# A hybrid layer on one core: earlier raw weight loads, a second state-space input buffer in dead norm roots, other unit spacing, and a down projection that loads one product ahead

## The chip, the core and the metric

The kernel runs on one core of one Trainium2 chip. The metric is the device time of one execution in microseconds (us); several executions are timed and their median is given. The engines are TensorE (PE, its weight loads PEld), VectorE (DVE), ScalarE (ACT), GpSimd (POOL) and SyncE (SP, whose queue issues most DMAs). GpSimd has a DMA queue too.

## What is computed

One layer of a hybrid encoder in float32, for 2048 frames of width 1024. A shared RMS norm feeds one input projection. Half of the mixer is a diagonal complex state-space layer (32 groups of 16 channels, 64 states each), the other half chunked attention with 8 heads, each 64-frame chunk looking at itself and 8 chunks before. Both halves are normalised, joined, projected and added to the residual; a SwiGLU feed-forward (width 2816) and a last norm follow.

```python
h = rmsnorm(x, norm_mix_g)
proj = h @ w_in                                  # u_ssm | q | k | v
y_ssm = s5_mixer(u_ssm, ...)                     # scan over time, then GELU and a sigmoid GLU
y_att = chunked_attention(q, k, v, rel_bias)
x = x + concat(rmsnorm(y_ssm, g1), rmsnorm(y_att, g2)) @ w_out
h2 = rmsnorm(x, norm_ffn_g)
x = x + (silu(h2 @ w_gate) * (h2 @ w_up)) @ w_down
return rmsnorm(x, norm_final_g)
```

## The kernel before

Every float32 product is made of three fp32r matmuls: each operand is split into a high part (a cast on ScalarE) and a low part (a subtraction on VectorE), `split` at L154, and `mm3` at L148 issues hi-hi, hi-lo and lo-hi. So weights that come from memory need a DMA, a cast and a subtraction before their first matmul. `Ordered` (L72) keeps TensorE's instructions in the order in which the program writes them; the other engines' instructions are placed by the framework, by dependence and priority, and each engine then runs its own list in order.

**Stages.** `u_phase` projects the state-space input u and stores it to memory; `att_phase` (L678) runs attention and, between its steps, the query, key and value projections and the state-space units; `mix_phase` (L967) applies GELU, GLU, norms and the output projection; `gate_up_phase` (L1337) and `down_phase` (L1475) are the feed-forward, done with seven products in place of eight per 2x2 block (`B11, T1, T2, B22, T3, B21, T4`).

**Attention's steps.** There are 128 steps (L905): four blocks of 512 frames, four head pairs, two heads, four query tiles. Each step issues scores (L823), the transposes of two steps ago (L855), now and then a product with V (L870), and advances every background unit (L940 to L959). A `Unit` (L656) is a generator with `n` pieces, a first step `s0` and a last `s1`; at each step `advance` (L663) runs so many pieces that the share done is the share of its steps gone, rounded up. `pre` lets a unit's first piece run that many steps ahead; the first piece is the one that loads weights. In block 0 the weights come raw (`load_w`, L684): a 512 KB DMA into one of two `raw` buffers, then `split` into one of three `w` buffers, both in the first piece; later blocks read the already split weights back (`ws`). Units of block 0 start at steps 2, 7, 13 and 19 (`CUT`, L51). GpSimd does only the state-space scan in this stage.

**State-space units** (`ssm_unit`, L557). Eight units of four groups each, 15 steps apart (`SW`, L50, L939), unit b from step 2 + 15b, so the last ends at 122. A unit has 42 pieces. The first loads its input U (eight DMAs of 64 KB, tile `U`, one buffer), `Bst`, eight `Tm` and `Vm` on SyncE (L563 to L577), then passes YL = 8 empty pieces. Two pieces do the input matmuls `pj<-U,Bst` (L585) and eight ScalarE copies into the scan's tile `X` (L588). GpSimd runs the scan (L602 to L614) and moves the states to `XG` with four DMAs (L636). After YX = 9 more empty pieces, two pieces do the output matmuls `pj<-U,Tm` and `pj<-XG,Vm` (L644, L645), which read U again; ScalarE copies the result to Y, which has the same tag and buffer as `X` (L639, L646), and SyncE stores it with eight DMAs (L649). The next unit's U, Tm and Vm can be loaded only after these output matmuls, and its copies into X only after the y stores.

**The norm roots** `rsn` (L1622) are a constant tile of 2048 columns. Columns 0 to 511 are read by block 0's projections (L762), 512 to 1023 by the transposed input of block 1 (L727), at steps 20 to 26; the mix writes it anew (L1211).

**Into the mix.** At step 119 (`OPEN`) the mix's generator is made and loads w_glu (L982); at step 122 (`GSTART`, L946) the state-space pool is released and the mix unit loads y (`yr<-y`, L1024), applies GELU on ScalarE (L1028), splits it (L1031) and begins the GLU matmuls (L1051).

**Down projection.** `group` (L1497) takes up to three feed-forward tiles and runs the seven products in turn. For each it loads two operands of 768 KB on SyncE and splits them (`operand`, L1487; ten `hd` buffers in two pools that lie where feed-forward tiles were), does twelve `mm3` triples (36 matmuls) in four banks and adds the four banks onto accumulators (L1513). The accumulators start as the residual x1: `load_acc` (L1515) loads eight tiles of 512 KB on SyncE, all of them after the operands of the first product. `early` gives the first two products of the first group a high priority. Just before, SyncE's queue carries the stores `hs<-g` of the feed-forward's last tiles (L1434), each of which waits for VectorE.

Of the kernel before, what the change touches and what calls it, by code (L numbers as in the profile page):

```python
# [16 lines left out]
P = 128  # L17
# [5 lines left out]
L = 8  # L23
# [35 lines left out]
MAGIC = 12582912.0  # L59
# [12 lines left out]
class Ordered:  # L72


    def __init__(self, tc):
        self.tc = tc
# [20 lines left out]
def f32(ap):  # L97
    return ap.bitcast(F32)
# [455 lines left out]
    return nb  # L554


def ssm_unit(k, p, psum, S, b, eng):  # L557

    nc = k.nc
    F = GB * CH  # L560
    U = k.t(p, "U", [P, GB, NC])

    def load(out, in_):  # L563
        ins = nc.sync.dma_start(out, in_)
        if b == 0:
            k.tc.keep_in_program_order(ins)

    for j in range(L):
        load(U[j * CH : (j + 1) * CH].rearrange("c g (n t) -> c g n t", n=NSB), S["u"].rearrange("(c g) n j t -> c g n j t", c=CH)[:, GB * b : GB * b + GB, :, j])
    gs = slice(GB * b, GB * b + GB)  # L570
    bst = k.t(p, "Bst", [P, GB, P])
    load(bst[:].rearrange("p g m -> p (g m)"), S["bst"][b // 2][:, (b % 2) * GB * P : (b % 2 + 1) * GB * P])
# [83 lines left out]
class Unit:  # L656


    def __init__(self, gen, n, s0, s1, pre=0, done=0, light=1):
        self.gen, self.n, self.s0, self.s1, self.pre, self.done = gen, n, s0, s1, pre, done  # L660
        self.room = lambda a, b: sum(light if s % 4 == LPH else 1 for s in range(a, b))

    def advance(self, s):  # L663

        if s < self.s0 - self.pre:
            return
        want = 1
        if s >= self.s0:
            want += math.ceil((self.n - 1) * self.room(self.s0, s + 1) / self.room(self.s0, self.s1) - 1e-9)
        if s >= self.s1 - 1:  # L670
            want = self.n + 1
        while self.done < want:
            self.done += 1
            if next(self.gen, self) is self:
                self.done = 1 << 30


def att_phase(k, ident, S, aw, x0, roots):  # L678

    tc, nc, io, pfs = k.tc, k.nc, k.io, k.pfs  # L680
    with ExitStack() as cx:
        hT, vts, qk, keep = {0: tuple(zip(*x0))}, {}, {}, {}

        def load_w(sb, n):  # L684

            w = k.t(aw, "w", [P, 2, 1024], F32R, bufs=WB)
            if sb == 0:
                raw = k.t(aw, "raw", [P, 1024], bufs=2)
                nc.sync.dma_start(raw[:], io["w_qk"][n] if n < 8 else io["w_v"][n - 8])
                for ins in split(k, w[:, 0], w[:, 1], raw[:]):  # L690
                    if n in (0, 4):
                        k.tc.keep_in_program_order(ins)
                keep[n] = w
            else:
                nc.sync.dma_start(f32(w[:]), S["ws"][n])
            return w[:, 0], w[:, 1]

        def keep_w(n):
            if n in keep:
# [30 lines left out]
            yield  # L730

        def qk_unit(sb, pr):
            ws = [load_w(sb, n) for n in (pr, 4 + pr)]
            yield
            hi, lo = hT[sb]
            if (sb, pr) == (0, 0):
# [43 lines left out]
        QK_N = 1 + 2 * KT  # L780

        def v_unit(sb, fh):
            ws = [load_w(sb, 8 + 2 * r + fh) for r in range(2)]
# [143 lines left out]
        for sb in range(NSB):  # L927
            g0 = sb * 32
            C = CUT if sb < NSB - 1 else CUTL
            if sb > 0:  # L930
                if DB:
                    units.append(Unit(hT_unit(sb, 0, DB), 2 + DB, g0 + HTA[0], g0 + HTA[1], 2))
                units += [Unit(hT_unit(sb, DB), 2 + KT - DB, g0 + HTS[0], g0 + HTS[1], HTP), Unit(qk_unit(sb, 0), QK_N, g0 + C[0], g0 + C[1], 3, light=LIGHT)]
            units.append(Unit(v_unit(sb, 0), V_N, g0 + C[1], g0 + C[2], 2, light=LIGHT) if sb else Unit(v0, V_N, *V0, done=1))
            units += [ Unit(qk_unit(sb, 1), QK_N, g0 + C[2], g0 + C[3], 2, light=LIGHT),
                      Unit(qk_unit(sb, 2), QK_N, g0 + C[3], g0 + C[4], 2, light=LIGHT), Unit(v_unit(sb, 1), V_N, g0 + C[4], g0 + C[5], 2, light=LIGHT),
                      Unit(qk_unit(sb, 3), QK_N, g0 + C[5], g0 + C[6], 2, light=LIGHT)]
# [537 lines left out]
def down_phase(k, S):  # L1475
    tc, nc, io = k.tc, k.nc, k.io
    V, te = nc.vector, k.te
    with ExitStack() as cx:
# [5 lines left out]
        def bank(pool):  # L1484
            return k.t(pool, "ps", [P, 512])

        def operand(src, early=False):  # L1487

            g, n = src.shape[0], src.shape[2]
            t = k.t(next(ring), "hd", [P, 2 * DG * 512], F32R)  # L1490
            hi, lo = (t[:, m * g * n : (m + 1) * g * n].rearrange("p (g c) -> p g c", g=g) for m in range(2))
            with tc.high_priority() if early else ExitStack():
                nc.sync.dma_start(f32(lo), src.rearrange("g p c -> p g c"))
            split(k, hi, lo, f32(lo))
            return hi, lo

        def group(hf, f0, g, acc, early):  # L1497

            fs = slice(f0, f0 + g)
            x, y = [bank(dx) for _ in range(4)], None  # L1500
            for n, on_x, first, r, c in ((B11, 1, 1, 0, 0), (T1, 0, 1, 1, 1), (T2, 1, 0, 0, 1), (B22, 0, 0, 0, 1), (T3, 1, 0, 1, 1), (B21, 0, 1, 0, 0), (T4, 1, 0, 1, 0)):
                h = operand(S["hq"][hf, fs, n], early and n in (B11, T1))
                w = operand(S["wc"][fs, n], early and n in (B11, T1))
                if n == B11 and f0 == 0:
                    load_acc(hf, acc)
# [9 lines left out]
        def load_acc(hf, acc):  # L1515
            for i in range(KT):
                a = k.t((a0, a1)[hf], f"acc{i}", [P, HALF])
                nc.sync.dma_start(a[:], S["x1"][i * P : (i + 1) * P, hf * HALF : (hf + 1) * HALF])
                acc.append(a)

        def down(hs, ds, tiles, acc, t0, tn, end):

# [174 lines left out]
```

## Time and profile before

| | |
|---|---|
| timed runs | 2287.0, 2295.97, 2296.15 us, median 2295.97 |
| the profiled execution | 2289.1 us |
| its span, first to last instruction | 2287.1 us, 2.0 us less |
| mean granted TensorE clock | 0.978 |
| moved by DMA | 428.33 MB, 187 GB/s over the span |
| state-space units | between 138 and 700 us |
| passage into the mix | 698 to 716 us |
| feed-forward's end and start of down | about 1830 us |

Times in the profile are microseconds from the span's start. A timeline row gives start, duration, engine, line, operation and `out<-in` by tile names, then a count, and in brackets how long the engine was idle before it and what released it. A row of the waits gives who waited for whom: total, times, longest. "SPq" is SyncE's queue. The releaser named is the last of several by the profile, not always the one that mattered. A row of the windows gives the stretch, its length, busy time of each engine with its count, then TensorE's granted clock, the share of the 16 DMA engines that was busy, and GB/s.

### The profile page before, as it was taken

Reading aid. Unit: us, or ns where it says so; the run is one execution under the profiler, and the core shown is the slowest. Engines: PE = TensorE matmul, PEld = TensorE weight load, DVE = VectorE, ACT = ScalarE, POOL = GpSimd, SP = SyncE. Lnnn points to the kernel's source line nnn. Section 1 sums busy time; section 2 is a strip of 40 time slices with the busy share of each in tenths; the row PEclk is TensorE's granted clock in tenths of the full one; section 3 lists DMA queues with packets and bytes.
Section 4 is the critical chain, followed back from the end, with each engine's and each line's share of the span. In section 5 each row is a group of like instructions: output and inputs, shape, how many; then the busy total and the mean of one; then the engine's idle time right before and its main releaser. Section 6 shows DMA issues by size and latency. Waiting matters only on the chain.

```text
span 2287.1 us, 30278 instructions
## 1 busy us (share of the span) xinstructions
PE 2171.6 (95%) x10632; PEld 1830.1 (80%) x10632; DVE 1544.7 (68%) x2695; ACT 1000.6 (44%) x1654; POOL 348.7 (15%) x813
## 2 busy tenths in 40 slices
PE   8988899999996899999999999999999989999997
PEld 6777688898985788878888887888888778888886
DVE  7755565555556766876776678666666477789776
ACT  6444555455557652343333335333333343344322
POOL 2245765455660000000000000000000000000000
PEclk9998999999998999999999999999999999999999
DMA  8767886666644534854465567555423297465552
GB/s 299 236 221 220 257 223 201 187 188 179 188 132 124 171 121 147 267 189 151 160 200 178 167 211 258 203 169 188 139 96 110 78 341 252 166 212 193 206 189 74
DMA packets 215256, 428.33 MB, mean 187 GB/s; under 512 B 38592, under 2 KB 61168, under 8 KB 208000
## 3 DMA queue, kind: packets, MB, share of 16 engines
q1 hardware_dynamic: 210368, 412.50, 55.3%
q0 software_dynamic: 4736, 13.91, 2.0%
q8 instruction: 83, 1.36, 0.2%
q14 instruction: 69, 0.57, 0.1%
HBM read 286.86 MB, written 129.00 MB: 182 GB/s over the span
## 4 chain that ended last, share of the span: by engine, by line
PE 80%; DVE 6%; DMA 4%; POOL 4%; issue 3%; ACT 1%; SPq 1%; DVEq 0%; POOLq 0%; ACTq 0%
PE X L79 20%; PE ps L79 19%; PE Y L79 10%; PE pf L79 9%; PE big L79 9%; PE W L79 5%; PE pj L79 4%; PE sc L79 2%; PE pt L82 2%; DMA xt<-in_xp 1%; DMA hd<-wc 1%; POOL X L605 1%; DVE lo L156 1%; POOL X L604 1%; POOL st L602 1%
## 5 line engine op out<-in xcount | busy, mean ns | idle before, releaser
L79 PE MATMUL X<-hi,c 128*128 128x512 f32 x1408 | 451.0, 391 | 6.9 <-DVE c L156 5.4
L79 PE MATMUL ps<-hd,hd 128*128 128x512 f32 (+1 forms) x1968 | 430.8, 381 | 6.1 <-ACT hd L156 4.5
L79 PEld LDWEIGHTS ps<-hd,hd 128*128 128x128 f32 x1968 | 358.0, 189 | 77.7 <-ACT hd L156 5.3
L79 PEld LDWEIGHTS X<-hi,c 128*128 128x128 f32 x1408 | 265.3, 189 | 63.4 <-DVE c L156 6.3
L79 PE MATMUL X<-lo,c 128*128 128x512 f32 x704 | 274.9, 391 | 0.0
L156 ACT CAST hd<-hd 128x1536 fp32r<-128x1536 f32 (+1 forms) x106 | 147.7, 1393 | 236.3 <-DMA hd<-hq 178.7
L79 PE MATMUL Y<-hi,c 128*128 128x512 f32 x704 | 224.7, 390 | 1.5 <-DVE u L1389 1.5
L156 DVE TENSOR_TENSOR hd<-hd 128x1536 fp32r<-128x1536 f32 (+1 forms) x106 | 174.4, 1646 | 29.1 <-ACT hd L156 28.4
L156 DVE TENSOR_TENSOR c<-S,c 128x512 fp32r<-128x512 f32 x176 | 121.0, 689 | 98.3 <-ACT c L156 98.0
L1385 ACT COPY u<-X 128x512 f32<-128x512 f32 x132 | 77.4, 587 | 200.7 <-PE X L79 200.7
L1513 DVE TENSOR_TENSOR acc<-acc,ps 128x512 f32<-128x512 f32 x196 | 130.9, 684 | 50.3 <-PE ps L79 47.8
L156 ACT CAST c<-S 128x512 fp32r<-128x512 f32 x176 | 109.4, 622 | 120.1 <-PE Y L79 61.6
L79 PE MATMUL pf<-hi,w 128*128 128x512 f32 x416 | 153.9, 422 | 8.4 <-ACT w L156 4.7
L79 PE MATMUL big<-m,woh 128*128 128x512 f32 x512 | 161.2, 396 | 0.0
L79 PEld LDWEIGHTS Y<-hi,c 128*128 128x128 f32 x704 | 132.5, 188 | 29.9 <-DVE u L1389 2.2
L79 PEld LDWEIGHTS X<-lo,c 128*128 128x128 f32 x704 | 132.8, 189 | 27.5
L156 ACT CAST c<-raw 128x512 fp32r<-128x512 f32 x132 | 82.3, 623 | 150.5 <-PE Y L79 68.5
L79 PE MATMUL Y<-lo,c 128*128 128x512 f32 x352 | 137.2, 390 | 0.0
L868 DVE TENSOR_TENSOR ptl<-pt,pth 128x640 fp32r<-128x640 f32 (+3 forms) x152 | 98.3, 647 | 47.5 <-ACT pth L867 45.9
L852 ACT ACTIVATE s<-s,mn 128x640 f32<-128x640 f32 (+4 forms) x128 | 98.0, 765 | 65.6 <-DVE mn L849 61.1
L867 ACT CAST pth<-pt 128x640 fp32r<-128x640 f32 (+3 forms) x152 | 83.8, 551 | 95.6 <-PE pt L82 91.5
L79 PE MATMUL W<-hi,c 128*128 128x512 f32 x352 | 115.5, 389 | 0.0
(441 smaller groups left out, 4169.9 us busy)
## 6 DMA issues: line engine op xcount, KB each, us to landing
w<-wss SPq DMA_DIRECT2D x36, 1024.0 KB, 6.0
hq<-g SPq DMA_DIRECT2D x140, 256.0 KB, 2.1
hd<-hq SPq DMA_DIRECT2D x42, 768.0 KB, 4.5
hd<-wc SPq DMA_DIRECT2D x42, 768.0 KB, 6.0
raw<-in_w_gate SPq DMA_DIRECT2D x44, 512.0 KB, 3.8
raw<-in_w_up SPq DMA_DIRECT2D x44, 512.0 KB, 4.3
wc<-px SPq DMA_DIRECT2D x66, 256.0 KB, 3.2
wss<-w SPq DMA_DIRECT2D x12, 1024.0 KB, 5.7
```

The costliest lines, as they stand in the source:

```text
L79: return self.tc.keep_in_program_order(self.tc.nc.tensor.matmul(*a, **b))
L82: return self.tc.keep_in_program_order(self.tc.nc.tensor.transpose(*a, **b))
L156: return nc.scalar.copy(hi, raw), nc.vector.tensor_tensor(lo, raw, f32(hi), op=ALU.subtract)
L602: eng.tensor_tensor(t[:, :, :, :n], src, ar, op=ALU.mult)
L604: eng.tensor_tensor(dst, dst, t[:, :, :, :n], op=ALU.add)
L605: eng.tensor_tensor(dst, dst, t2[:, :, :, :n], op=ALU.add)
L852: nc.scalar.activation(s[:, :nk], s[:, :nk], AF.Exp, bias=mn[:], scale=-1.0, accum_out=sums[sb, pr][:, hh, qp : qp + 1])
L867: nc.scalar.copy(pth[:, a:b, qp, :], pt[:, a:b, :])
L868: nc.vector.tensor_tensor(ptl[:, a:b, qp, :], pt[:, a:b, :], f32(pth[:, a:b, qp, :]), op=ALU.subtract)
L1385: nc.scalar.copy(u[:], ps[:])
L1513: V.tensor_tensor(a, a, ps[:], op=ALU.add)
```

## The change

Four things, in the order of the diff.

1. **Spacing.** The units start at the steps in `SU`; the last ends at 119. From unit 2 on, four of the eight empty pieces ahead of the input matmuls are moved behind the scan (`YE`), so that a unit still has 42 pieces.
2. **State-space input.** `ssm_input` loads U and Bst. Units 2, 4 and 6 keep U in `rsn`, the others in tile `U`. For units 2 to 7 it is called from the unit before, two pieces after its XG DMAs; units 0 and 1 load at their own start as before.
3. **Raw weights.** In block 0 the units after the first two issue both raw DMAs four steps ahead (`pre` 4) and split two steps ahead (`mid` 2), where both were done two steps ahead.
4. **Down projection.** In a half's first group the operands of product m + 1 are loaded before the matmuls of product m. In the very first group they are issued on GpSimd's queue (`aside`). The residual comes in quarters (`load_acc(hf, acc, r, c)`, four DMAs of 256 KB), each ahead of the first product that adds to it.

```diff
-SW = 15
+SU = 2, 19, 34, 48, 62, 76, 91, 105, 119
+YE = 4
...
+def ssm_input(k, p, S, b):
+
+    U = S["rsn"][:, : GB * NC].rearrange("p (g c) -> p g c", g=GB) if b > 1 and b % 2 == 0 else k.t(p, "U", [P, GB, NC])[:]
+    bst = k.t(p, "Bst", [P, GB, P])
+    for j in range(L):
+        src = S["u"].rearrange("(c g) n j t -> c g n j t", c=CH)[:, GB * b : GB * b + GB, :, j]
+        yield U[j * CH : (j + 1) * CH].rearrange("c g (n t) -> c g n t", n=NSB), src
+    yield bst[:].rearrange("p g m -> p (g m)"), S["bst"][b // 2][:, (b % 2) * GB * P : (b % 2 + 1) * GB * P]
+    k.ssm_in = U, bst
...
-    for j in range(L):
...
+    if b < 2:
+        for out, src in ssm_input(k, p, S, b):
+            load(out, src)
+    U, bst = k.ssm_in
...
-    for _ in range(YL):
+    for _ in range(YL if b < 2 else YL - YE):
         yield
...
-    for _ in range(YX):
+    for n in range(YX if b < 2 else YX + YE):
+        if n == 2 and 1 <= b < NG // GB - 1:
+            for out, src in ssm_input(k, p, S, b + 1):
+                nc.sync.dma_start(out, src)
         yield
...
-        want = 1
+        want = 1 if self.mid is None or s < self.s0 - self.mid else 2
         if s >= self.s0:
-            want += math.ceil((self.n - 1) * self.room(self.s0, s + 1) / self.room(self.s0, self.s1) - 1e-9)
+            want += math.ceil((self.n - want) * self.room(self.s0, s + 1) / self.room(self.s0, self.s1) - 1e-9)
...
+        def load_ws(sb, ns):
+            raws = [load_raw(n) for n in ns] if sb == 0 else []
+            if raws and ns not in ((0, 4), (8, 10)):
+                yield
+            ws = []
+            for i, n in enumerate(ns):
+                w = k.t(aw, "w", [P, 2, 1024], F32R, bufs=WB)
+                if raws:
+                    for ins in split(k, w[:, 0], w[:, 1], raws[i][:]):
...
-            units += [ Unit(qk_unit(sb, 1), QK_N, g0 + C[2], g0 + C[3], 2, light=LIGHT),
...
+            for gen, n, c in ((qk_unit(sb, 1), QK_N, 2), (qk_unit(sb, 2), QK_N, 3), (v_unit(sb, 1), V_N, 4), (qk_unit(sb, 3), QK_N, 5)):
+                units.append(Unit(gen, n, g0 + C[c], g0 + C[c + 1], 2, light=LIGHT) if sb else Unit(gen, n + 1, C[c], C[c + 1], 4, light=LIGHT, mid=2))
         for b in range(NG // GB):
-            units.append(Unit(ssm_unit(k, sp, psum, S, b, k.ssm_eng), SSM_N, 2 + int(SW * b), 2 + int(SW * (b + 1)), light=SL))
+            units.append(Unit(ssm_unit(k, sp, psum, S, b, k.ssm_eng), SSM_N, SU[b], SU[b + 1], light=SL))
...
-                nc.sync.dma_start(f32(lo), src.rearrange("g p c -> p g c"))
+                (nc.gpsimd if aside else nc.sync).dma_start(f32(lo), src.rearrange("g p c -> p g c"))
...
+            if f0 == 0:
+                acc += [k.t((a0, a1)[hf], f"acc{i}", [P, HALF]) for i in range(KT)]
+                load(0)
+            seen = set()
+            for m, (n, on_x, first, r, c) in enumerate(order):
+                load(m + 1 if f0 == 0 else m)
+                if f0 == 0 and (r, c) not in seen:
+                    seen.add((r, c))
+                    load_acc(hf, acc, r, c)
+                h, w = ops.pop(n)
...
+        def load_acc(hf, acc, r, c):
+            for i in range(4 * r, 4 * r + 4):
+                cs = slice(hf * HALF + c * 512, hf * HALF + (c + 1) * 512)
+                nc.sync.dma_start(acc[i][:, c * 512 : (c + 1) * 512], S["x1"][i * P : (i + 1) * P, cs])
```

More of the change, by code (lines that the diff above doesn't have):

```diff
@@ L560, in ssm_unit @@
     F = GB * CH
-    U = k.t(p, "U", [P, GB, NC])
     def load(out, in_):
@@ L656, with __init__ @@
 class Unit:
-    def __init__(self, gen, n, s0, s1, pre=0, done=0, light=1):
-        self.gen, self.n, self.s0, self.s1, self.pre, self.done = gen, n, s0, s1, pre, done
+    def __init__(self, gen, n, s0, s1, pre=0, done=0, light=1, mid=None):
+        self.gen, self.n, self.s0, self.s1, self.pre, self.done, self.mid = gen, n, s0, s1, pre, done, mid
         self.room = lambda a, b: sum(light if s % 4 == LPH else 1 for s in range(a, b))
@@ L682, in att_phase, with load_raw @@
         hT, vts, qk, keep = {0: tuple(zip(*x0))}, {}, {}, {}
[L684 to L696, printed above, removed]
+        def load_raw(n):
+            raw = k.t(aw, "raw", [P, 1024], bufs=2)
+            nc.sync.dma_start(raw[:], io["w_qk"][n] if n < 8 else io["w_v"][n - 8])
+            return raw
+        def load_ws(sb, ns):
[7 more added lines that the diff above has]
+                    for ins in split(k, w[:, 0], w[:, 1], raws[i][:]):
+                        if n in (0, 4):
+                            k.tc.keep_in_program_order(ins)
+                    keep[n] = w
+                else:
+                    nc.sync.dma_start(f32(w[:]), S["ws"][n])
+                ws.append((w[:, 0], w[:, 1]))
+            return ws
         def keep_w(n):
@@ L732, in qk_unit @@
         def qk_unit(sb, pr):
-            ws = [load_w(sb, n) for n in (pr, 4 + pr)]
+            ws = yield from load_ws(sb, (pr, 4 + pr))
             yield
@@ L782, in v_unit @@
         def v_unit(sb, fh):
-            ws = [load_w(sb, 8 + 2 * r + fh) for r in range(2)]
+            ws = yield from load_ws(sb, (8 + fh, 10 + fh))
             yield
@@ L1485, in bank, with operand @@
             return k.t(pool, "ps", [P, 512])
-        def operand(src, early=False):
+        def operand(src, early=False, aside=False):
             g, n = src.shape[0], src.shape[2]
@@ L1499, in group, with load @@
             fs = slice(f0, f0 + g)
+            order = (B11, 1, 1, 0, 0), (T1, 0, 1, 1, 1), (T2, 1, 0, 0, 1), (B22, 0, 0, 0, 1), (T3, 1, 0, 1, 1), (B21, 0, 1, 0, 0), (T4, 1, 0, 1, 0)
             x, y = [bank(dx) for _ in range(4)], None
[L1501 to L1505, printed above, removed]
+            ops = {}
+            def load(m):
+                if m < len(order):
+                    n = order[m][0]
+                    soon = early and n in (B11, T1)
+                    ops[n] = operand(S["hq"][hf, fs, n], soon, early), operand(S["wc"][fs, n], soon, early)
+            if f0 == 0:
[8 more added lines that the diff above has]
+                h, w = ops.pop(n)
                 if not on_x and first:
@@ L1513, in group @@
                     V.tensor_tensor(a, a, ps[:], op=ALU.add)
[L1515 to L1519, printed above, removed]
+        def load_acc(hf, acc, r, c):
+            for i in range(4 * r, 4 * r + 4):
+                cs = slice(hf * HALF + c * 512, hf * HALF + (c + 1) * 512)
+                nc.sync.dma_start(acc[i][:, c * 512 : (c + 1) * 512], S["x1"][i * P : (i + 1) * P, cs])
         def down(hs, ds, tiles, acc, t0, tn, end):
```

5 lines of the change are left out of this document (removed).

## The prediction

> **What bounds the kernel now.** I read the page first, for how much of the span TensorE is busy.
>
> ```profile
> span 2287.1 us, 30278 instructions
> ...
> PE 2171.6 (95%) x10632; PEld 1830.1 (80%) x10632; DVE 1544.7 (68%) x2695; ACT 1000.6 (44%) x1654; POOL 348.7 (15%) x813
> ```
>
> TensorE (PE) is idle for 2287.1 - 2171.6 = 115.5 us. The change takes no matmul away, so it can win only idle time and time at a lowered clock. Next I cut the span into windows around the longest idle stretches. The columns used are the window, its length, the granted TensorE clock (third from the end) and the DMA engines' share and rate (last two).
>
> ```profile
> 173.01:190.15 17.14, 17.09 (x74) 13.84 (x74) 9.82 (x20) 7.68 (x19) 15.42 (x45) 0.83 0.67 228
> 193.50:210.84 17.34, 16.96 (x103) 15.32 (x103) 10.23 (x25) 8.98 (x24) 12.18 (x16) 0.83 0.82 256
> 638.83:652.00 13.17, 9.44 (x53) 8.71 (x54) 3.37 (x6) 5.48 (x14) 4.35 (x9) 0.87 0.61 167
> 699.02:714.56 15.54, 3.67 (x15) 2.92 (x14) 5.95 (x11) 10.68 (x14) 0.00 (x0) 0.57 0.81 263
> 1816.90:1822.49 5.59, 5.59 (x25) 4.31 (x23) 1.38 (x2) 0.59 (x1) 0.00 (x0) 1.00 0.07 27
> 1822.49:1862.00 39.51, 31.94 (x125) 24.76 (x126) 25.56 (x24) 16.84 (x12) 0.00 (x0) 0.91 1.02 384
> ```
>
> A window after a long wait has a clock under 1, and a busy window of length T at clock c loses about T(1-c). The four edits touch four places in these windows: attention's first block (to 296 us), the later state-space units (296 to 650), the passage into the mix (698 to 716) and the start of the down projection (1824 to 1862). I take each by its list of TensorE's waits: total, times, longest.
>
> **First block: raw weights two steps earlier, units 0 and 1 spread over 17 and 15 steps.**
>
> ```profile
> PE pt L82 <- DVE ptl L868: 5.2, 3, 3.4
> PE pf L79 <- ACT w L156: 4.7, 1, 4.7
> PE pj L79 <- DMA XG<-X: 1.7, 1, 1.7
> ```
>
> The 4.7 us is the split of query/key weights (head pair 2 of block 0) whose raw load and split were issued together, two steps ahead; now the load goes two steps earlier on SyncE, past rotations and key stores, and finds its two raw buffers free; the longest of the first row, 3.4, is a transpose behind two such weight splits on VectorE. Each is followed by a slow window: 17.14 x 0.17 = 2.9 and 17.34 x 0.17 = 2.9. If nothing else were late, earlier raw loads would win 4.7 + 3.4 + 5.8 = 13.9 us. But something is: the scan on GpSimd. Its chain stands in TensorE's and GpSimd's timelines.
>
> ```profile
> 158.61 1.89 PE L79 MATMUL pj<-U,Bst 128*128 128x256 f32 x8
> ...
> 212.53 0.67 PE L79 MATMUL pj<-XG,Vm 128*128 128x256 f32 x2 [1.68 <-DMA XG<-X]
> ...
> 227.11 1.97 PE L79 MATMUL pj<-U,Bst 128*128 128x256 f32 x8 [1.45 <-DMA Tm<-kts]
> ...
> 281.66 0.67 PE L79 MATMUL pj<-XG,Vm 128*128 128x256 f32 x2 [1.94 <-DMA XG<-X]
> ```
> ```profile
> 162.85 0.51 POOL L602 TENSOR_TENSOR st<-X,a 128x128 f32<-128x128 f32 x1 [24.00 <-ACT X L588]
> ```
>
> Unit 0's input matmuls at 158.61 (step 4) start the scan, and TensorE waits for its result, XG, at 212.53 (step 16): 12 steps of (212.53 - 158.61)/12 = 4.5 us. Unit 1's input at 227.11 waits for unit 0's output, because they share one U buffer; that stays so for b < 2. The link 212.53 to 227.11 is 14.6 us, the next scan 227.11 to 281.66 is 54.6 us. This chain doesn't shorten when TensorE gets its weights earlier.
>
> Now the spacing. A unit has 42 pieces and is advanced by 41k/(its steps), rounded up. With 17 steps instead of 15 the second half of unit 0's input comes at step 5 instead of 4: 4.5 us later, less about a third of the 162.85 - 158.61 = 4.2 us between input and scan, the first half's copies, which run meanwhile; the scan starts 3 us later. Its output moves from step 16 to 18. Chain after: XG at 212.5 + 3 = 215.5, unit 1's input at 230.1, its XG at 284.7, the output matmuls done 2.9 us later (as 212.53 to 215.44 in this trace, an estimate of mine) at 287.6, the end of step 33. Before, step 31 ends at 281.66 + 2.9 = 284.6 and step 33 two steps later, at 293.6. So the block ends **6 us** earlier, not 13.9: TensorE arrives early and waits for XG instead. Two such waits of about 5 us each bring a slow window as above; I take 3 us off for that. Term: **-3 us** (from +2, if both slow windows cost 2.9 and a third wait comes, to -9, if the half of unit 0 that slips costs nothing).
>
> [...]
>
> **Later units: U and Bst loaded ahead, U alternating between its tile and `rsn`.**
>
> ```profile
> PE pj L79 <- DMA Tm<-kts: 9.7, 3, 3.7
> PE sc L79 <- DVE k L775: 5.2, 2, 3.1
> PE pt L82 <- DVE ptl L868: 3.8, 1, 3.8
> ```
> ```profile
> 632.08 3.94 SPq L649 DMA_DIRECT2D y<-X  x8
> 636.12 0.36 SPq L902 DMA_DIRECT2D ya_s<-ya  x1
> 636.52 3.53 SPq L564 DMA_DIRECT2D U<-u  x7
> ```
>
> The first row is three waits of input matmuls (units 2, 3 and 7). The row names Tm, but these matmuls read only U and Bst: SyncE's queue shows why they wait, with eight y stores and then the U loads, one after the other, after the previous unit's output. With U in a second buffer the nine loads are issued about four steps (18 us) earlier; SyncE then issues nine DMAs of some 3.53/7 = 0.5 us at a place where no U is due, and their buffers have long been free, so nothing is held behind them. So 9.7 us go, and with the last of them 13.17 x 0.13 = 1.7 us of clock: 11.4 us.
>
> What is late next is the scan's tile X, still one buffer and also the tile of the output Y: the copies into it must wait for the y stores, and for b >= 2 the input now comes one step earlier after them (4 pieces ahead of it, not 8).
>
> ```profile
> y<-X SPq DMA_DIRECT2D x64, 64.0 KB, 2.1
> ```
>
> At unit 7 the last y store is issued at 632.08 + 3.94 = 636.0 and lands at 638.1. TensorE reached the input at 638.83 (the third window's start); a step less makes it 634.3, so ScalarE's copy would wait up to 3.8 us, with the exponentials and casts of attention queued behind it, and TensorE waits for those. The other five boundaries have their y stores earlier in relation; between nothing and 6 x 3.8 = 23 us I take 3 us, near the low end, because only unit 7's stores were held up in the queue. Term: 11.4 - 3 = **-8 us** (from -11.4 to +11.6). The rest of the two other rows (attention's own splits) isn't touched.
>
> **Into the mix: the last unit ends at step 119, not 122.**
>
> ```profile
> PE pf L79 <- ACT gh L156: 6.8, 1, 6.8
> PE pt L82 <- DVE ptl L868: 5.1, 2, 3.4
> ```
> ```profile
> 696.72 3.62 SPq L649 DMA_DIRECT2D y<-X  x8
> 702.86 0.34 SPq L902 DMA_DIRECT2D ya_s<-ya  x1
> 703.43 0.53 SPq L1024 DMA_DIRECT2D yr<-y  x1
> ```
>
> The last yr load waits for the last y stores; GELU, its split and the first GLU matmul hang on it, and TensorE's 15.54 us window holds 3.67 us of work. Three steps earlier, y is there before yr is asked for. But the second row, transposes behind w_glu's splits, stays, and the output matmuls (2.9 us) leave an idle place for one where TensorE is busy. Of 6.8 us I count all, less 2.9: **-4 us** (from 0 to -10, if the clock of 0.57 recovers as well).
>
> **Down projection: operands one product ahead, on GpSimd's queue; residual in quarters.**
>
> ```profile
> PE ps L79 <- ACT hd L156: 4.5, 2, 2.7
> PE ps L79 <- DVE hd L156: 1.6, 2, 1.1
> ```
> ```profile
> 1821.25 0.32 SPq L1434 DMA_DIRECT2D hs<-g  x1
> 1821.66 0.39 SPq L1493 DMA_DIRECT2D hd<-hq  x1
> ...
> 1824.64 6.80 SPq L1434 DMA_DIRECT2D hs<-g  x3
> 1831.56 5.88 SPq L1518 DMA_DIRECT2D acc<-x  x8
> 1837.58 0.44 SPq L1493 DMA_DIRECT2D hd<-hq  x1
> ```
>
> The first operand load sits behind an hs store that waits for VectorE (1821.25), the third product's behind three hs stores and all 4 MB of residual (1837.58). From 1822 to 1862 the DMA engines are full (1.02, 384 GB/s), but in the 5.6 us before they are at 0.07. On GpSimd's queue, empty here, the first two loads start as their buffers come free, and the third product's wait for none of the stores; only 1 MB of residual per quarter is due with each product. I count both rows, 6.1 us, and of the clock's 39.51 x 0.09 = 3.6 us about 2: **-8 us** (from -9.7 to -4). The group's fourteen loads from GpSimd's queue have no row here; with the engines full they land at best as fast as SyncE's, and -4 is the end at which the third product's stay late. Sixteen residual DMAs instead of eight cost SyncE 8 x 5.88/8 = 5.9 us more of issuing, hidden while it has nothing else due.
>
> [...]
>
> **Sum**: -3 - 8 - 4 - 8 = -23 us. The profiled execution took 2289.1 us (span 2287.1), so 2266.1. The median of the three timed runs, 2295.97, is 6.9 us above that execution, the lowest, 2287.0, 2.1 below; I forecast **2266**, and leave the 6.9 to the upper end of the range.
>
> **Rivals.**
> - All stalls go (10%): the scan isn't late and the slow windows vanish: 13.9 + 11.4 + 10 + 9.7 = 45, about 2244. For it: GpSimd is 15% busy. Against it: the two XG waits, which exist already.
> - The order is only moved (15%): XG waits swallow the first block, DMA interleaving keeps half the down stalls: 0 + 4 + 0 + 4 = 8 us: 2281 from the profiled execution, 2288 from the median, which is within 0.5% of it. [...]
> - Slower (9%): the single X buffer. The place is ScalarE's copy L588 at six boundaries, the price 6W for a hold of W us. The other terms win 15 + 11.4 = 26.4; it is slower by 0.5% from W = (26.4 + 11.5)/6 = 6.3 us, and W = 8 gives 2289.1 + 48 - 26.4 = 2310.7. For it: the y stores queue on SyncE behind rotations and bias loads. Against it: 3.8 us is the most that I can read.
>
> **Numbers.** 0.5% (about 11.5 us) is what a measurement of this kernel can tell from no change. Forecast 66%, the three rivals as above. Range: low end 2245, the all-stalls case; high end 2290, the moved-order case plus 6.9 us and a little of the X hold. Faster than 2284.5: 66 + 10 = 76%; same 15%; slower 9%.
>
> **What would show it.** No input-matmul wait in units 2 to 7; XG waits of units 0 and 1 longer than 1.7 and 1.9 us; first-block end 3 to 6 us earlier; L588 beginning within 2 us of its matmul; yr's last load before 700; no wait between the first three down products. I am wrong in the mechanism if XG waits don't grow while the w wait goes, or if TensorE waits for ptl and pth just after each new input.

## The result, and the profile after

The changed kernel takes 2314.84 us (median of four runs, 2308.15 to 2315.03) against 2296.06 us for the kernel before in the same comparison: a ratio of 1.0084, interval 1.0059 to 1.0109. It is **slower by 0.8%**, some 19 us; I had forecast 2266 and a range up to 2290. The profiled execution took 2314.96 us.

First the page of the kernel after: span, then TensorE's row.

```profile
span 2313.1 us, 30299 instructions
...
PE 2178.3 (94%) x10632; PEld 1835.2 (79%) x10632; DVE 1544.1 (67%) x2695; ACT 1002.1 (43%) x1654; POOL 360.9 (16%) x827
```

The matmuls are the same 10632; TensorE is idle for 2313.1 - 2178.3 = 134.8 us, where it was 115.5. To find the place I cut both spans at the same steps: attention's 0, 36, 120 and 127 (the starts of the maskings of scores on VectorE, one for each step), and at the last stores of the feed-forward. The work between two cuts is nearly the same (2244 and 2241 matmuls in the second row), not quite, because the units' pieces fall at other steps. The windows of before, then of after; the columns are as in the prediction.

```profile
136.00:307.40 171.40, 145.65 (x812) 125.78 (x813) 91.31 (x209) 86.05 (x215) 86.31 (x192) 0.92 0.76 224
307.40:688.40 381.00, 363.99 (x2244) 331.17 (x2242) 220.19 (x384) 207.42 (x411) 216.36 (x523) 0.97 0.64 186
688.40:732.10 43.70, 28.01 (x146) 23.60 (x146) 23.27 (x52) 29.78 (x42) 0.00 (x0) 0.80 0.53 157
732.10:1822.49 1090.39, 1074.23 (x4779) 887.58 (x4777) 752.19 (x1277) 440.31 (x722) 0.00 (x0) 0.99 0.50 166
1822.49:2287.10 464.61, 442.33 (x2048) 368.59 (x2048) 354.23 (x474) 170.13 (x151) 0.00 (x0) 0.98 0.58 206
```
```profile
134.00:307.00 173.00, 146.16 (x823) 127.50 (x823) 90.78 (x207) 84.20 (x211) 85.15 (x185) 0.91 0.71 214
307.00:720.10 413.10, 375.94 (x2241) 337.72 (x2241) 222.53 (x388) 211.84 (x420) 218.79 (x528) 0.95 0.60 177
720.10:763.20 43.10, 27.10 (x134) 22.13 (x135) 22.69 (x52) 28.24 (x39) 0.00 (x0) 0.76 0.47 143
763.20:1853.32 1090.12, 1072.09 (x4779) 886.15 (x4776) 751.60 (x1277) 440.60 (x722) 3.08 (x4) 0.99 0.50 168
1853.32:2313.10 459.78, 440.32 (x2049) 367.97 (x2048) 353.07 (x474) 169.62 (x151) 7.60 (x10) 0.99 0.58 204
```

The loss is in the second row, steps 36 to 120: 413.1 against 381.0, **32.1 us** more. TensorE is idle there for 413.10 - 375.94 = 37.2 us, before for 381.00 - 363.99 = 17.0: 20.2 us of the loss; the granted clock is 0.95 against 0.97, worth 375.94 x 0.05 - 363.99 x 0.03 = 7.9 us more; the remaining 4 us lie within the clock's two digits (0.005 of 376 us is 1.9 us, in each row). The first block ends at step 36 no earlier to speak of (307.0 against 307.4), the passage into the mix is as long as before, the down projection is 4.8 us shorter. What TensorE waits for in the second stretch, after:

```profile
PE pj L80 <- ACT X L599: 10.7, 3, 4.1
PE sc L80 <- DVE mn L871: 10.2, 7, 3.7
PE pj L83 <- ACT X L599: 4.6, 1, 4.6
PE pf L80 <- DMA w<-wss: 4.2, 4, 2.3
```

The input waits `pj <- Tm<-kts` of before (9.7 us) are gone, as forecast. In their place stand 15.3 us behind ScalarE's copies into X (L588 before, L599 now), 10.2 behind the minimum of the masked scores (1.1 before), and 4.2 behind weights of the later blocks, which TensorE never waited for in before's stretch. The masks themselves wait 6.9 us on VectorE for their biases, DMAs `nba<-nbs` and `nbb<-nbs` of SyncE's list, which they never waited for in before: so weights are not the only loads that come late. (Lines of the changed kernel are shifted; in the experiments below the same weight load is L709 or L716.)

Three theories came out of this. **X**: the copies into X are held, because X is still owed to the y stores. **Q**, later sharpened to **L**: the nine loads ahead sit in SyncE's in-order list and put other loads late. **P**: the steps at which the units' pieces now fall are bad ones.

### The profile page after: what moved, and what is told of

It reads as the page before. It is cut to its first block, busy times and chain, and to the rows that moved or that the text cites. A ratio compares the mean times of both kernels' runs of the same rounds, so it can differ in the third digit from the quotient of the medians.

```text
span 2313.1 us, 30299 instructions
## 1 busy us (share of the span) xinstructions
PE 2178.3 (94%) x10632; PEld 1835.2 (79%) x10632; DVE 1544.1 (67%) x2695; ACT 1002.1 (43%) x1654; POOL 360.9 (16%) x827
## 4 chain that ended last, share of the span: by engine, by line
PE 79%; DVE 7%; DMA 6%; ACT 2%; issue 2%; SPq 2%; POOL 2%; DVEq 0%; ACTq 0%; POOLq 0%
PE X L80 20%; PE ps L80 17%; PE Y L80 10%; PE pf L80 9%; PE big L80 9%; PE W L80 5%; PE pj L80 4%; PE sc L80 2%; PE pt L83 2%; DMA w<-wss 1%; DMA xt<-in_xp 1%; DMA hd<-wc 1%; DMA lo<-hc 1%; SPq L575 1%; DVE ptl L890 0%
## 5 line engine op out<-in xcount | busy, mean ns | idle before, releaser
L1514 POOL DMA_DIRECT2D hd<-hq x7 | 5.3, 764 | 1147.1 <-PE X L80 1134.1
```

The lines of the kernel that those rows point to most:

```text
L1514: (nc.gpsimd if aside else nc.sync).dma_start(f32(lo), src.rearrange("g p c -> p g c"))
```

## Experiments

The unit of every comparison is the kernel before, run beside each experiment; ratios are with their 95% interval.

**1. Y over the unit's own U, in the changed kernel.** This takes away the reason for which X is held.

```diff
-    Y = k.t(p, "X", [P, GB, NC])
+    Y = U if b else k.t(p, "X", [P, GB, NC])
```

> The changed kernel, with one thing different: from unit 1 on the output Y is written over the unit's own U and no longer into the scan's tile X, so that nothing makes ScalarE's copies into X wait for the y stores. Theory X (the copies into X are held, by the y stores or by a place in ScalarE's list behind exponentials that come later, and TensorE waits for the bank they read: 3.3 + 3.3 + 4.1 + 4.6 us, with slow windows after them): the copies start within about 2 us of their matmuls, the four waits of TensorE for L599 go, and 25 to 35 us are won over the changed kernel: 2280 to 2290 us, 0.2 to 0.7% faster than before. Theory Q (the loss is in SyncE's queue, where the nine loads of U and Bst for the next unit stand between weight loads and key stores and are themselves held, so that later weights come late): the waits for w<-wss stay, less than 10 us are won, 2305 us or more.

Measured: 2313.5 us, ratio 1.0098 (1.0071 to 1.0126): nothing is won. Yet the waits for L599 did go, as theory X had it; that less than 10 us were won is what theory Q expected. TensorE's waits in this kernel, 296 to 720 us:

```profile
PE sc L80 <- DVE mn L871: 14.4, 8, 3.9
PE pf L80 <- DMA w<-wss: 11.2, 3, 8.0
```

L599 fell from 15.3 to 0.6 us (two rows of 0.4 and 0.2), and the wait for weights rose from 4.2 to 11.2, that for the minimum from 10.2 to 14.4. So X alone isn't the cause; a second one took its place.

**2 to 4. One part at a time.** Each is the kernel before with one part of the diff: the down projection; the raw weights; the state-space part (spacing, four pieces, loads ahead).

> The kernel before, with the down projection's part of the change alone. The changed kernel's trace has its waits at the start of the down projection at 1.8 us where there were 6.1, and by its times from there on it wins 5 us of those lost before. If parts add up: 4 to 8 us faster, 2288 to 2292 against 2296. If what the down projection won came only from its later start in the changed kernel: no difference.

> The kernel before, with the earlier raw weight loads alone. My prediction's step (the scan's chain is late next, XG then makes TensorE wait): the wait for w of 4.7 us goes, the wait for XG grows from 1.7 us towards 5, and the whole is 0 to 4 us faster. Theory that the first block's gain is real once the units keep their old spacing: 8 to 14 us faster, 2282 to 2288. Theory that the loads get in the way of others on SyncE: slower.

> The kernel before, with the state-space part alone (spacing, four pieces moved, U and Bst loaded ahead). If the loss is all here, as theories X and Q both have it: 20 to 30 us slower, 2316 to 2326, with the same waits for L599. If the loss comes from the parts together (raw loads that move the steps against the units): within 10 us of before.

Measured: down projection 2284.21 us, 0.9973 (0.9958 to 0.9988), about 6 us faster. Raw weights 2294.47 us, 1.0020 (1.0003 to 1.0037), some 4 us slower where I expected 0 to 4 us faster: no gain. State-space part 2318.99 us, 1.0124 (1.0097 to 1.0151), 28 us slower, with the same waits for L599 (10.7 and 4.6) as the whole change. The loss is in the state-space part.

**5 to 8. The state-space part taken apart.** Before with (5) the loads ahead at the old 15 steps; (6) that and the four pieces moved; (7) the spacing alone, U loaded at the unit's start; (8) as 5 with the down projection. The edits are `SU = 2, 17, 32, 47, 62, 77, 92, 107, 122` and `YE = 0` or `YE = 4` in the changed code; for 7 `YE = 0`, `ssm_input` called at each unit's own start and U always in its tile.

> The kernel before, with U and Bst loaded ahead into the second buffer and nothing else: units stay 15 steps apart, eight empty pieces stay ahead of the input. In ScalarE's list the copies into X stand behind the same number of exponentials as before, but for unit 3, where it is one more. Theory P (the places: the loss comes from the steps at which the units' pieces now fall, and loading ahead is harmless): the three input waits of 9.7 us go and it is 4 to 12 us faster than before. Theory Q (nine more loads in SyncE's queue in a busy place hold weights, biases and y stores): 5 to 20 us slower, with waits for w<-wss.

> As the last, and four empty pieces moved from ahead of the input to behind the scan, so that the input comes a step earlier; units still 15 steps apart. In ScalarE's list the copies into X of units 2, 3, 5, 6 and 7 now stand behind one exponential more than the scores that TensorE has issued before the input. Theory X (copies held): TensorE waits 3 to 4.5 us for L599 at up to five units, 10 to 20 us slower than the run without the move. Theory that only the 14-step spacing hurts: as the run without the move.

> The kernel before, with only the units' first steps changed (2, 19, 34, 48, 62, 76, 91, 105, end at 119); U and Bst load at their unit's start into the one buffer, eight empty pieces ahead of the input. No copy into X stands behind a later exponential. Theory P (the places decide: output matmuls and their copies fall into steps in which key or value weights change, and scores wait for the exponential's minimum): 15 to 25 us slower than before. Theory X or Q: within 8 us of before, since nothing is loaded ahead and no copy is held; U waits of some 10 us stay or grow.

> The kernel before, with U and Bst loaded ahead at the old spacing, and the down projection's part. If parts add up: the down projection's 6 us and what loading ahead brings alone, 10 to 18 us faster than before if theory P is right, and 6 us better than the run without the down projection's part in any case.

Measured: (5) 2310.93 us, **1.0075** (1.0052 to 1.0099); (6) 2327.44 us, **1.0143** (1.0122 to 1.0164); (7) 2302.72 us, 1.0038 (1.0022 to 1.0053); (8) 2304.06 us, 1.0045 (1.0029 to 1.0062). Loading ahead, which I had priced as pure gain, costs 17 us by itself; the four pieces cost another 16 on top of it; the spacing alone costs 9, between the 15 to 25 of theory P and the 8 of X and Q; the down projection's gain adds up (0.9973 x 1.0075 = 1.0048 against 1.0045). The three costs do not: 17, 16 and 9 make 42, and the whole part costs 28 (4). In the trace of 7 the waits of the inputs grow from 9.7 to 14.7 us (8.4 of them at unit 7) and that for gh from 6.8 to 10.6.

Why does loading ahead cost? SyncE's queue around the start of unit 7, first in before, then in experiment 5:

```profile
611.26 0.33 SPq L695 DMA_DIRECT2D w<-wss  x1
...
620.19 0.33 SPq L695 DMA_DIRECT2D w<-wss  x1
...
632.08 3.94 SPq L649 DMA_DIRECT2D y<-X  x8
```
```profile
628.81 1.96 SPq L651 DMA_DIRECT2D U<-u  x4
...
649.30 3.86 SPq L663 DMA_DIRECT2D y<-X  x8
653.26 0.37 SPq L916 DMA_DIRECT2D ya_s<-ya  x1
653.67 0.93 SPq L709 DMA_DIRECT2D w<-wss  x2
654.65 9.50 SPq L575 DMA_DIRECT2D Tm<-kts  x8
```

In before the two 1 MB weights of the next projection are issued one by one, as their buffers come free, 12 and 21 us ahead of the y stores. With the U loads in the list the framework wrote the two weight loads behind the y stores, which wait for the output matmuls; SyncE issues them without a pause behind these stores, so what they waited for was their place in the list. TensorE then stood still for 6.1 us (its waits from 625 to 670):

```profile
PE pf L80 <- DMA w<-wss: 6.4, 2, 6.1
```

Counted over the whole list of the built kernel: ahead of the y stores of units 1 to 6 stand 5, 11, 17, 23, 28 and 34 of the later blocks' weight loads in before, and 4, 10, 16, 22, 26 and 32 in experiment 5. That is theory L: what costs is not the loads' traffic, but the new **order of the list**. Experiments 9 to 17 try it.

The four pieces of experiment 6 act on ScalarE's list (in the table below the waits for X grow by 7.7 us from 5 to 6, those for weights by 4.1). Before each unit's copies into X stand, in before, as many exponentials as scores were issued before its input (5, 20, 35, 50, 65, 80, 95, 110). In experiment 6 it is one more at units 2, 5, 6 and 7 and two at unit 3, in the changed kernel one more at units 3, 5 and 7 and two at unit 6. Here is what that looks like in the changed kernel at unit 3, SyncE, TensorE and ScalarE:

```profile
354.62 3.61 SPq L663 DMA_DIRECT2D y<-X  x8
```
```profile
360.95 1.89 PE L80 MATMUL pj<-U,Bst 128*128 128x256 f32 x8
362.48 0.50 PE L80 MATMUL sc<-k,q2h 128*128 128x320 f32 x1
...
366.75 0.50 PE L80 MATMUL pj<-pth,v 128*128 128x512 f32 x1 [3.33 <-ACT X L599]
```
```profile
364.39 0.83 ACT L874 ACTIVATE s<-s,mn 128x640 f32<-128x640 f32 x1 [3.24 <-DVE mn L871]
365.12 0.19 ACT L874 ACTIVATION_READ_ACCUMULATOR s<-s,mn 128x1 f32 x1
365.21 3.01 ACT L599 COPY X<-pj 64x256 f32<-64x256 f32 x8
```

The last y store was issued by 358.2 and landed at 359.9, before the input begins: X is free. Still the copies wait, for the exponential listed ahead of them, whose scores TensorE issues only after the input (362.48). Meanwhile both `pj` banks are full, and the product with V has to wait 3.33 us for one. At units 5 and 6 (3.33 and 4.07 us) the copies stand behind a later exponential in the same way. At unit 7, the longest, they do not wait for the exponential but for X itself, as the prediction had it, SyncE first and then ScalarE:

```profile
648.67 3.12 SPq L663 DMA_DIRECT2D y<-X  x7
658.60 0.34 SPq L765 DMA_DIRECT2D k<-ks  x1
658.98 0.43 SPq L663 DMA_DIRECT2D y<-X  x1
```
```profile
661.61 3.03 ACT L599 COPY X<-pj 64x256 f32<-64x256 f32 x8 [1.21 <-issue]
```

The eighth y store is issued 7.6 us after the seventh, behind a key load that waits; it landed at 661.54, and the copies begin 0.07 us later, 5.5 us after the input matmuls began (656.10).

**9 to 12. Loads ahead on GpSimd's queue; then Y over U as well.** (9) is 5 with `eng.dma_start` (GpSimd) in place of `nc.sync.dma_start` for the loads ahead; (10) the whole change with that; (11) the whole change with that and with Y over U; (12) before's spacing with loads ahead on GpSimd, Y over U and the down projection's part.

```diff
             for out, src in ssm_input(k, p, S, b + 1):
-                nc.sync.dma_start(out, src)
+                eng.dma_start(out, src)
```

> The kernel before with U and Bst loaded ahead at the old spacing, as in the run that cost 17 us (0.75%), but issued on GpSimd's queue. Theory L (the order of SyncE's list: with the nine loads in it, the framework put one or two of the 1 MB weight loads of later blocks behind the y stores of the unit before, 4, 10, 16, 22, 26 and 32 ahead of the stores of units 1 to 6 where before had 5, 11, 17, 23, 28 and 34; out of SyncE's list the counts are those of before again): the waits for w<-wss go, and it is within 4 us of before or up to 12 us faster. Theory R (the loads themselves, by their traffic or their time, get in the way): still 10 us or more slower. Known against a full win: the copies into X of units 3 and 7 stand behind one exponential more, 3 to 5 us each.

> The whole change, with the loads ahead on GpSimd's queue. Theory L: the weights stand ahead of the y stores as in the run with the spacing alone, and 8 to 15 us are won over the changed kernel (which was 19 to 22 slower than before): 0.2 to 0.5% slower than before. What remains is the copies into X, listed behind one or two later exponentials at units 2, 3, 5, 6 and 7. Theory R: as the changed kernel, 0.8 to 1.0% slower.

> As the last, and the output Y is written over the unit's own U, so that no copy into X stands behind a later exponential. Theories L and X together (two causes, each hidden by the other when mended alone): 15 to 25 us won over the changed kernel, from 0.2% faster to 0.2% slower than before. If Y in U wins nothing here either, copies into X cost nothing: as the last run.

> The kernel before at its old spacing, with U and Bst loaded ahead on GpSimd's queue, Y over U, and the down projection's part. Both lists are as before's in the counts above. Theories L and X: the down projection's 6 to 7 us and most of the 9.7 us of input waits: 10 to 18 us faster than before (0.4 to 0.8%). Theory R: 5 us slower or more.

Measured: (9) 2297.01 us, 1.0032 (1.0011 to 1.0053): 10 us of the 17 are gone, but it isn't ahead of before; it lies between theory L (within 4 us) and theory R (10 or more). (10) 2304.68 us, 1.0056 (1.0037 to 1.0075). (11) 2290.86 us, **0.9998** (0.9984 to 1.0013). (12) 2281.78 us, **0.9955** (0.9936 to 0.9973), faster than both kernels. TensorE's waits for X's copies in 9 (300 to 700 us), then for weights in 11 (290 to 690 us):

```profile
PE pj L80 <- ACT X L599: 6.8, 2, 3.5
```
```profile
PE pf L80 <- DMA w<-wss: 6.3, 1, 6.3
```

In 9 the weights are never waited for, as the mended list has it (5, 11, 17, 23, 28 and 34 of them ahead of the y stores, as in before). What is left is X and one wait of 4.8 us for which the profile names nobody, ahead of the matmuls `pj<-XG,Vm` of unit 5 (568.58). With Y over U no copy into X is listed behind a later exponential any more, at any unit. The two causes hid each other: mending X alone won nothing (1), mending the list alone 0.3% at most (10, whose interval overlaps the changed kernel's), both won 0.9% (11). The rows of six kernels side by side, in us between 296 and 700:

| kernel | wait for w<-wss | wait for X's copies | ratio |
|---|---|---|---|
| changed | 4.2 | 15.3 | 1.0084 |
| 1: Y over U | 11.2 | 0.6 | 1.0098 |
| 5: ahead only | 10.9 | 3.5 | 1.0075 |
| 6: ahead, four pieces | 15.0 | 11.2 | 1.0143 |
| 10: changed, GpSimd | none | 15.7 | 1.0056 |
| 11: changed, GpSimd, Y over U | 6.3 | 0.6 | 0.9998 |

**13, 14, 16 and 17. What stayed open.** Is it the list's order, or SyncE's queue as such? (16) keeps the loads ahead on SyncE, with Y over U, and gives the later weight loads a high priority; (17) is its control, before with that priority alone. And what do spacing (13) and the four pieces (14) cost in the mended kernel 12?

```diff
-                nc.sync.dma_start(f32(w[:]), S["ws"][n])
+                with k.tc.high_priority():
+                    nc.sync.dma_start(f32(w[:]), S["ws"][n])
```

> The kernel before at its old spacing, with U and Bst loaded ahead on SyncE's queue, where they cost 17 us, Y over U, and the later blocks' weight loads at high priority, so that the framework lists them early: 5, 11, 17, 23, 28 and 35 weight loads ahead of the y stores of units 1 to 6, as in before or one more. Theory L (the order of the list is what cost): within 5 us of before, or faster. Theory that SyncE's queue cannot take nine more loads, in whatever order: 8 us slower or more.

> The control: the kernel before with the later blocks' weight loads at high priority and nothing else. In before TensorE never waits for w<-wss in the later units, so both theories expect no difference (within 4 us); if it is faster or slower by more, the run with the loads ahead must be read against this one.

> As the run with GpSimd's loads, Y over U and the down projection (0.45% faster than before), with the changed kernel's spacing (ends at step 119; eight pieces stay ahead of the input). Theory L for the end of the stage: the last unit's y stores now stand ahead of two of the four w_glu loads in SyncE's list and hold them, so the wait for gh is 10.6 us where it was 8.1, and a weight load behind unit 6's y stores costs TensorE some 6 us: 5 to 10 us slower than that run. My prediction's step (ending at 119 wins 4 us at the passage): 4 us faster than that run.

> As the run with GpSimd's loads, Y over U and the down projection, with four empty pieces moved behind the scan, at the old spacing. No copy into X stands behind a later exponential and the weights keep their places. Theory X (those four pieces cost 16 us only by the copies): within 5 us of that run. If an earlier input costs by itself: 8 us slower or more.

Measured: (16) 2331.07 us, 1.0171 (1.0147 to 1.0195), and its control (17) 2330.93 us, 1.0170 (1.0151 to 1.0188). Both theories expected nothing of the control, and it lost 39 us: with no other edit than the priority of weight loads, these now stand early in SyncE's list and wait there for buffers (127.4 us in 31 waits for TensorE's matmuls from 290 to 725 us), and the U loads behind them come late. TensorE's first wait in 17 (290 to 690 us), then the first in 16 (296 to 700 us) and what VectorE's masks wait for there:

```profile
PE pj L79 <- DMA Tm<-kts: 31.0, 5, 9.1
```
```profile
PE sc L80 <- DVE mn L864: 33.7, 10, 9.0
```
```profile
DVE s L864 <- DMA nbb<-nbs: 21.0, 4, 6.6
```

The two have nearly the same time (1.0171 and 1.0170) and lose it at different places: in 17 the input loads are late, in 16, where these are loaded ahead, it is the bias loads behind the waiting weights. So their difference doesn't tell what nine more loads cost on SyncE, and whether its queue could take them in a good order stays open. That such a re-ordering of the list can cost more than the whole change did is shown. (14) 2283.74 us, 0.9964 (0.9950 to 0.9977): as 12, so the four pieces are free once both causes are mended. (13) 2305.0 us, 1.0051 (1.0031 to 1.0072), against 0.9955 for 12: the spacing costs about 1% of its own in the mended kernel, 22 us where I expected 5 to 10. Its waits from 290 to 720 us:

```profile
PE pf L80 <- ACT gh L157: 10.6, 1, 10.6
PE pt L83 <- DVE ptl L882: 8.7, 8, 2.8
PE pj L80 <- DMA XG<-X: 8.0, 3, 5.9
PE pf L80 <- DMA w<-wss: 5.4, 1, 5.4
```

With units of 14 steps and eight pieces still ahead of the input, the scan is too late for its output (XG 8.0 us); with four (experiment 11) that wait is 0.2 us. For that wait the pieces are worth their place; 11 also has the raw weights, which alone won nothing, so the 0.5% between the two isn't split further.

## Why the prediction was wrong, step by step

- **Later units (-8): the step that failed**, and with it the sign. I wrote of the loads ahead that their buffers have long been free, "so nothing is held behind them". I priced the instructions and left their neighbours where they were. But the list of SyncE isn't the program's: the framework writes it anew, and it put one or two 1 MB weight loads per unit behind the y stores. Alone that cost 17 us (0.75%) where I had a gain of 11.4; 10 of them went when the loads left SyncE's list. Why the framework chose this order no run shows. The gain was mis-sized too: with both causes mended and the old spacing (12), loading ahead (with Y over U) is worth 4 us over the down projection alone (0.9955 against 0.9973, with overlapping intervals). The three input waits are gone there (9.9 us in 2, from 296 to 690), but those for the minimum rise from 1.9 to 6.1 and those for the transposes from 3.2 to 4.8.
- **The X hold (+3, bounds 0 to 23)** was right in kind and mis-sized: 15.3 us of waits at four places (3.3, 3.3, 4.1 and 4.6), and four pieces that cost 16 us on top of the loads ahead. I read the price from when y stores land and so found "3.8 us is the most". At unit 7 the store was indeed what held X: it landed 5.4 us after the input matmuls began, in before 4.8 us ahead of them. At units 3, 5 and 6 the copies were late by their place in ScalarE's list, which no landing time shows. The third rival, "Slower", was this mechanism at 9%, but it wasn't enough either: without X's waits the change is still 0.98% slower.
- **First block (-3)**: right in the mechanism, nothing in the sum. The wait for w is gone (a transpose still waits 3.3 us for ptl) and XG swallows it, at unit 0 in one wait in place of two of 5; at unit 1 there is none:

```profile
217.33 1.19 PE L80 MATMUL pj<-XG,Vm 128*128 128x256 f32 x2 [9.19 <-DMA XG<-X]
```

  The raw weights alone have the same at 6.2 us, with units at their old spacing, so some 3 us of the 9.2 seem to go with the new places of units 0 and 1. Step 36 comes at 307.0 against 307.4, and 1.6 us later when counted from step 0.
- **Into the mix (-4)** failed. The wait for gh grew from 6.8 to 10.6 us. SyncE after, at the passage:

```profile
709.83 0.85 SPq L1007 DMA_DIRECT2D sg<-in_w_glu  x2
...
718.01 3.61 SPq L663 DMA_DIRECT2D y<-X  x8
721.71 0.85 SPq L1007 DMA_DIRECT2D sg<-in_w_glu  x2
```

  In before all w_glu loads were issued by 692.5, ahead of the y stores at 696.72. With the last unit three steps earlier its y stores, which wait for the output, are listed ahead of two of the four. Every kernel with the new spacing (the change, 1, 4, 7, 10, 11, 13) waits 10.6 us for gh, those with the old one 6.8 to 8.1. But neither these loads nor y set that wait: the last w_glu load landed at 725.7, the yr loads were issued by 725.4 and took at most 6.8 us where a landing is recorded, and GELU begins at 740.21. What sets it is ScalarE's list, here from the last transposes' cast on, first in before, then after:

```profile
707.84 0.69 ACT L867 CAST pth<-pt 128x640 fp32r<-128x640 f32 x1 [1.20 <-PE pt L82]
708.55 1.28 ACT L1028 ACT_TABLE_LOAD   x1
```
```profile
734.98 1.14 ACT L157 CAST wgh<-sg 128x512 fp32r<-128x512 f32 x2
737.98 0.83 ACT L874 ACTIVATE s<-s,mn 128x640 f32<-128x640 f32 x1 [1.86 <-DVE mn L871]
738.92 1.28 ACT L1049 ACT_TABLE_LOAD   x1
```

  In before GELU's table load follows that cast at once. After, the casts of the two late w_glu pieces and one more exponential stand between; that exponential waits for a minimum which VectorE makes behind the same pieces' subtractions. From the cast's end (735.08) to the table load (738.92) it is 3.8 us, the whole growth of the wait. That the splits stand there because their loads are listed late is argued and not tried. In before, too, the last yr load was there (707.6) ahead of the table load, so GELU didn't wait for it; my sum had read it as the one that holds the mix.
- **Down projection (-8)**: held. The waits of 4.5 and 1.6 us became 2.0 in the part alone, and it is worth 6 us (0.27%). Its edits (one product ahead, GpSimd's queue, the residual in quarters) were made together, so which of them does it isn't shown.

```profile
PE ps L79 <- DVE hd L156: 2.0, 2, 1.8
```

- **The second rival** had DMA interleaving keep half of the down projection's stalls, 4 us. No run shows this term; alone, the part's 6.1 us of waits fell to 2.0. In the changed kernel the fourteen loads of 768 KB on GpSimd's queue landed in 10.1 us (`hd<-hq`) and 8.3 us (`hd<-wc`), medians of seven each, and the waits are 2.0 us as well. In experiment 9 nine loads of some 0.5 us per unit, moved to GpSimd's queue and otherwise the same, won 10 us (1.0075 to 1.0032): what was won is that other loads of SyncE's list came earlier (TensorE's wait for w<-wss is 10.9 us in 5, none in 9).

## What to carry to other kernels

Where a framework orders each engine's list, an added instruction is priced with the list that comes out: compare the built lists before and after, and count what now stands behind a waiting store or a later exponential. A tile with one buffer can hold its writer by its place in such a list long after it is free (5.3 us for X at unit 3 of the changed kernel). When mending one cause wins nothing, look at which wait took its place before giving the cause up: here the list's mend won 6 us at most, that of X nothing alone and 13 us after it.

## What the runs showed of the hardware

In the traces of the kernels before and after, SyncE's DMAs (1256 and 1258) signal eight semaphores in turn, and none is issued before the one eight places ahead of it has landed (936 and 938 pairs with a recorded landing, the closest 0.02 us apart in each). Whether the framework or the chip makes it so no run shows. In two places small DMAs right behind two 1 MB loads were slow. In the changed kernel eight y stores stretch over 9.88 us against 3.61 at unit 3; the eighth was issued at 505.68, when the second of these weights, eight places ahead of it, had landed (505.66):

```profile
495.02 0.97 SPq L716 DMA_DIRECT2D w<-wss  x2
496.10 9.88 SPq L663 DMA_DIRECT2D y<-X  x8
```

From issue to landing these y stores took up to 9.8 us, where the median of all 64 is 2.1. In experiment 5, behind the two weight loads issued from 653.67 on, the eight Tm loads of 32 KB stretch over 9.50 us against 3.73 at the same unit of before; the seventh was issued by 660.93 and the eighth by 664.15. So here a pair of late weight loads delayed not only itself: the small DMAs in the next places of the list were issued or landed late with it.
